# Expert weights of a two-layer mixture-of-experts trunk: three 1 MB transfers per expert, in rows of 8192 bytes, in place of six of 512 KB

## The chip, the cores and the metric

The kernel runs on 1 core of one Trainium2 chip. The metric is the device time of one execution in microseconds (us), median of several runs. One core has TensorE (PE, with its weight loads as PEld), VectorE (DVE), ScalarE (ACT), GpSimd (POOL), SyncE (SP, which here issues the plain DMA transfers) and 16 DMA engines that all queues share.

## The reference, cut to what matters

Two layers over 256 latent and 256 context tokens of width 1024. Each layer has a mixing part (a state-space layer, attention, an mLSTM) and a mixture of experts, which is the part that matters here:

```python
scores = sigmoid(h @ router_w)                  # 64 experts, 8 groups of 8
top_e  = top 8 experts of a token, out of its 4 best groups, by scores + router_bias
gate   = scores[top_e] / sum * 2.5
y      = sum over a token's 8 experts of  gate * ((silu(h @ w_gate[e]) * (h @ w_up[e])) @ w_down[e])
y     += shared expert (same form, for all tokens)
```

`w_gate` and `w_up` are 1024 x 256 per expert, `w_down` is 256 x 1024, all float32: 3 MB per expert (MB in sizes of transfers and slots means 2^20 bytes), 64 experts in each of the 2 layers. Layer 0 routes 512 tokens, layer 1 only the 256 latent ones.

## The kernel before, in words

**Weights in memory.** `prep` (line 101) packs each expert as [128 partitions, 6144]: for k = 0 to 7 the 512 columns of gate and up for the k-th 128 rows of the input, then two blocks of 1024 columns of the down projection. Line 162 cuts this into six chunks of [128, 1024], each contiguous: chunks 0 to 3 are gate and up (two k each), chunks 4 and 5 are down.

**The ring.** `moe` (line 1919) allocates `ring` (line 1931): slots of 4096 bytes per partition, so of 512 KB, 13 of them in layer 0 and 18 in layer 1. One transfer fills one slot. Transfers go round the slots in a fixed order: transfer q goes to slot q modulo the number of slots, and so has to wait until the use of transfer q minus that number is over.

**Units and ranks.** The program counts tokens per expert and sorts the experts by it; the r-th is "rank r". `plan` (line 203) fixes units of work over ranks, with letters in `ORDER` (line 169): X is one rank in two tiles of 128 rows; A, B and C are two ranks in two tiles; L one rank in one tile; D and M two ranks in one tile; S up to four ranks in one tile, 32 columns of the array each. The order, written by hand, is `MSLBCMCLLMLXDMDAXCAMSLMDXSALCBMXLDD` in layer 0 (35 units) and `BDMCSMSLXLMSCXDSCSSSMSLMSM` in layer 1 (26 units). Units are counted from 0 here (C17 is the C that is unit 17 of layer 0). A tile costs PE the same whether one expert or four share it, but an S needs four experts' bytes.

**Order of loads and of use.** `experts` (line 1692) lists the loads in `seq` (lines 1697 to 1702): for unit i all ranks' chunk 0, then chunk 1, and so on to 3, then chunks 4 and 5 of unit i-1. `load` (line 1706) issues the next of them on SP's queue, with the expert's number read into a register; beyond the first ring-full it is conditional on the expert having tokens. `start_loads` (line 1722) fills the ring at the start of the stage, and from then on `gate_up` (line 1777) and `down` (line 1790) call `load` once for each slot that they have used up.

**Order on PE.** For each unit (loop at line 1824): `gate_up` of unit i, the transposes of unit i+1's inputs (`transp`, line 1746), `down` of unit i-1, then the transposes of unit i's hidden values. In `gate_up`, one chunk of all of the unit's ranks is taken at a time (line 1781), and inside it PE goes over tiles, k and ranks; the `load`s for these slots follow the whole chunk. In `down`, PE takes chunks 4 and 5 of all ranks, and gives all their slots back after the last tile.

**Beside it.** In layer 0 the tokens' rows are gathered by indirect DMA on POOL's queue (`gather`, line 1734, two units ahead); in both layers `down` adds its result rows to `Y` in memory by indirect DMA (line 1808). `spilled` (line 1881) handles tokens over the planned capacities, in a loop that reads the ring as one expert's six chunks; its loop makes no pass on these inputs (the trace has 768 expert transfers, 384 per layer, which is 64 times 6).

Of the kernel before, what the change touches and what calls it, by code (L numbers as in the profile page):

```python
# [10 lines left out]
F32 = mybir.dt.float32  # L11
# [89 lines left out]
def prep(inp):  # L101
    f = {k: np.asarray(v) for k, v in inp.items()}
    L = DEPTH
    o = {}
# [54 lines left out]
        dn = np.moveaxis(wd.reshape(*lead, 2, 128, 1024), -3, -2).reshape(*lead, 128, 2048)  # L159
        return np.concatenate([gu, dn], -1)  # L160

    o["exp_w"] = pack(f["exp_w_gate"], f["exp_w_up"], f["exp_w_down"]).reshape(L * 64, 128, 6, 1024).transpose(0, 2, 1, 3)
    o["sh_w"] = pack(f["sh_w_gate"], f["sh_w_up"], f["sh_w_down"])
    o["cst"] = CST
    return {k: np.ascontiguousarray(v) for k, v in o.items()}
# [84 lines left out]
class Trunk:  # L250
# [1441 lines left out]
    def experts(self, l, units, mq, rp, ring, merge):  # L1692
# [3 lines left out]
        part = lambda u, cs: [(u, r, c) for c in cs for r in u["ranks"]]  # L1696
        seq = []
        for i, u in enumerate(units):
            seq += part(u, range(4))
            if i:  # L1700
                seq += part(units[i - 1], (4, 5))
        seq += part(units[-1], (4, 5))
        regs = {}
        state = dict(load=0, use=0)

        def load():
            q = state["load"]
            if q >= len(seq):
                return
            u, r, c = seq[q]  # L1710
            state["load"] += 1
            dst = ring[:, q % NR, :]
            if c == 0:
                vl = lambda at, mx, why: nc.values_load(self.idt[0:1, at:at + 1], engines=[ET.SP], min_val=0, max_val=mx,
                                                        skip_runtime_bounds_check_because=why)
                regs[r] = (vl(r, 63, "an expert's number"), vl(64 + r, 512, "a count of tokens") if q + 24 >= NR else None)
            e, n = regs[r]

            kw = {} if q < NR else dict(cond=n > 0)
            nc.sync.dma_start(dst, wt[l * 64:(l + 1) * 64][ds(e, 1), c].rearrange("e p f -> (e p) f"), **kw)  # L1720
# [56 lines left out]
        def gate_up(u):  # L1777
            for t in u["tiles"]:
                t["gu"] = self.bank("gu")
            for c in range(4):  # L1780
                ws = [use() for _ in u["ranks"]]
                for t in u["tiles"]:
                    for b in range(2):
                        for j, r, kw in pieces(u, t):
                            nc.tensor.matmul(t["gu"][r, :], t["xt"][:, 2 * c + b, r], ws[j][:, b * 512:(b + 1) * 512],  # L1785
                                             start=c == 0 and b == 0, stop=c == 3 and b == 1, **kw)
                for _ in ws:
                    load()

        def down(u):  # L1790
            nr = len(u["ranks"])
            ws = [use() for _ in range(2 * nr)]
            for t in u["tiles"]:
                po = [self.bank("dn") for _ in range(2)]
                for b in range(2):
                    for n in range(2):
                        for j, r, kw in pieces(u, t):
                            nc.tensor.matmul(po[n][r, :], t["ht"][:, b, r], ws[b * nr + j][:, n * 512:(n + 1) * 512],  # L1798
                                             start=b == 0, stop=b == 1, **kw)
                m = t["m"]  # L1800
                xo = rp.tile([128, D], F32, name="xo", bufs=4)
                nc.scalar.activation(xo[0:m, 0:512], po[0][0:m], AF.Identity, scale=t["gc"][0:m])  # L1802
                v.tensor_scalar(out=xo[0:m, 512:1024], in0=po[1][0:m], scalar1=t["gc"][0:m], scalar2=None, op0=OP.mult)  # L1803
                if l and u is units[-1]:
                    t["xo"] = xo
                    continue
                for (_, _, col, _, cap), si in zip(t["segs"], t["si"]):
                    nc.gpsimd.indirect_dma_start(out=self.Y[l], out_offset=bass.IndirectOffsetOnAxis(ap=si[0:cap], axis=0),  # L1808
                                                 in_=xo[col:col + cap], in_offset=None, compute_op=OP.add,
                                                 bounds_check=TOK[l] - 1, oob_is_err=False)  # L1810
            for _ in range(2 * nr):
                load()

        n = len(units)
# [66 lines left out]
    def spilled(self, l, fT, acc, sw, rp, ring, tiles):  # L1881
# [5 lines left out]
        with tc.For_i(0, n, 1) as q:  # L1887
            vl = lambda at, why: nc.values_load(self.ovl[0:1, ds(q + at, 1)] if at else self.ovl[0:1, ds(q, 1)], engines=[ET.SP], min_val=0,
                                                max_val=63, skip_runtime_bounds_check_because=why)
            e, r = vl(0, "an expert's number"), vl(64, "a rank")  # L1890
            w = ring[:, 0:6, :]
            for c in range(6):
                nc.sync.dma_start(w[:, c], d["exp_w"][l * 64:(l + 1) * 64][ds(e, 1), c].rearrange("e p f -> (e p) f"))
            co = rp.tile([128, nt], F32, name="spc")
            nc.sync.dma_start(co, self.cod[l][ds(r, 1), :nt * 128].rearrange("o (i p) -> (o p) i", p=128))
            for i in range(nt):
                gu = self.bank("gu")
                for k in range(8):
                    nc.tensor.matmul(gu, fT[:, k, i * 128:(i + 1) * 128], w[:, k // 2, (k % 2) * 512:(k % 2) * 512 + 512], start=k == 0, stop=k == 7)
                sg = rp.tile([128, 256], F32, name="sg", bufs=3)  # L1900
                h = rp.tile([128, 256], F32, name="hh", bufs=3)
                nc.scalar.activation(sg, gu[:, 0:256], AF.Silu)
                v.tensor_tensor(out=h, in0=gu[:, 256:512], in1=sg, op=OP.mult)
                ps = self.bank("hT")
                ht = rp.tile([128, 2, 128], F32, name="hT", bufs=4)
                for b in range(2):
                    self.tpose(ps[:, b * 128:(b + 1) * 128], h[:, b * 128:(b + 1) * 128])
                v.tensor_copy(ht, ps[:, 0:256].rearrange("p (b n) -> p b n", b=2))
                for n2 in range(2):
                    po = self.bank("dn")  # L1910
                    for b in range(2):
                        nc.tensor.matmul(po, ht[:, b], w[:, 4 + b, n2 * 512:(n2 + 1) * 512], start=b == 0, stop=b == 1)
                    a = acc[:, i, n2 * 512:(n2 + 1) * 512]
                    t = sw[:, 4 + n2, 0:512]
                    v.scalar_tensor_tensor(out=t, in0=po, scalar=co[:, i:i + 1], in1=sw[:, 2 if tiles[i] >= 2 else 3, n2 * 512:(n2 + 1) * 512],
                                           op0=OP.mult, op1=OP.mult)
                    v.tensor_tensor(out=a, in0=a, in1=t, op=OP.add)

    def moe(self, l, mq, fT, sw, lg, tiles, spare):
# [5 lines left out]
        with ExitStack() as es:  # L1925
            rp = es.enter_context(self.tc.tile_pool(name=f"moe{l}", bufs=1))
            if l == 0:
                self.xg = [rp.tile([128, D], F32, name=f"xg{i}") for i in range(5)]
                for x in self.xg:
                    nc.gpsimd.memset(x, 0.0)  # L1930
            ring = rp.tile([128, 18 if last else 13, 1024], F32, name="ring")
            self.xn = 0
            merge = self.merging(l, acc, sw, spare, tiles)
            for i, t in enumerate(tiles[:3]):
# [98 lines left out]
```

## Time and profile before

| | us |
|---|---|
| median of 3 runs | 1990.86 (1983.97 to 1991.81) |
| the profiled execution's own time | 1989.93 |
| its span in the profile | 1988.1 |
| PE busy | 1802.0 (91%) |
| PEld busy | 851.0 (43%) |
| DVE, ACT, POOL busy | 813.2, 379.5, 456.1 |
| DMA over the span | 524.16 MB, mean 264 GB/s |

The expert stage of layer 0 runs from about 392 us (first load issued) to 1085 us, that of layer 1 from about 1428 us to 1948 us. PE's busy time is a union of matmul durations; matmuls of different 32-column groups overlap, so the same busy time can hold more or less work. The share of DMA is the time that packets took, over 16 engines; it can pass 100%, as packets on one engine overlap a little.

### The profile page before, as it was taken

What the parts mean: (1) busy time and instruction counts of PE and PEld (TensorE: products, weight loads), DVE (VectorE), ACT (ScalarE), POOL (GpSimd) and SP (SyncE); (2) the same over time, 40 slices, a digit from 0 to 9 for tenths busy, and PEclk for the clock granted to TensorE, in tenths of its full rate; (3) what the DMA queues carried; (4) which work ended last, traced back from release to release, by engine and by line L of the source; (5) the groups of instructions that cost most, each with busy time, mean ns of one, the idle gap of its engine ahead of it and who ended that gap; (6) DMA issues with size and microseconds to landing.
All of it is one profiled execution on the core that took longest, in us unless ns stands there. A gap on an engine that the chain in (4) does not pass through costs nothing. (4 is left out here: it accounts for less than half of the span.)

```text
span 1988.1 us, 29110 instructions
## 1 busy us (share of the span) xinstructions
PE 1802.0 (91%) x10161; PEld 851.0 (43%) x10161; DVE 813.2 (41%) x2298; ACT 379.5 (19%) x739; POOL 456.1 (23%) x453
## 2 busy tenths in 40 slices
PE   6998999879999999899997178899899999999992
PEld 2554665523334333233332055665543354433340
DVE  6856664731223432222121598764731222312113
ACT  2245331201111111001111313341301011110000
POOL 3120211232223232332221551002101211111223
PEclk7999999989999999999999588999999999999996
DMA  8442567399999999999997423256499999899672
GB/s 321 140 96 101 178 250 293 116 319 358 298 326 340 360 323 293 386 377 339 344 297 232 163 75 64 75 213 258 182 372 343 398 353 358 304 385 355 234 261 69
DMA packets 153922, 524.16 MB, mean 264 GB/s; under 512 B 28787, under 2 KB 37939, under 8 KB 145068
## 3 DMA queue, kind: packets, MB, share of 16 engines
q1 hardware_dynamic: 135228, 480.36, 65.1%
q0 software_dynamic: 18544, 41.90, 9.5%
q8 instruction: 82, 1.34, 0.3%
q14 instruction: 68, 0.56, 0.1%
HBM read 531.12 MB, written 47.61 MB: 291 GB/s over the span
## 5 line engine op out<-in xcount | busy, mean ns | idle before, releaser
L1785 PE MATMUL gu<-ring,xT 128*32 128x512 f32 (+5 forms) x2896 | 645.7, 602 | 18.2 <-DMA ring<-in_exp_w 17.7
L1785 PEld LDWEIGHTS gu<-ring,xT 128*32 128x32 f32 (+5 forms) x2896 | 193.7, 129 | 399.3 <-issue 321.2
L1798 PE MATMUL dn<-ring,hT 128*32 128x512 f32 (+5 forms) x1448 | 330.0, 597 | 4.8 <-DMA ring<-in_exp_w 4.0
L1808 POOL DMA_INDIRECT Y<-xo,gi x79 | 119.9, 1518 | 610.8 <-DMA Y<-xo,gi 140.5
L1681 DVE TENSOR_TENSOR hh<-gu,sg 128x256 f32<-128x256 f32 (+4 forms) x86 | 36.5, 424 | 523.2 <-ACT sg L1680 503.7
L1798 PEld LDWEIGHTS dn<-ring,hT 128*32 128x32 f32 (+5 forms) x1448 | 103.1, 128 | 183.2 <-issue 155.7
L1808 POOL DMA_INDIRECT Y<-xo,si x66 | 91.0, 1379 | 302.6 <-DMA Y<-xo,gi 217.4
L1803 DVE TENSOR_SCALAR xo<-dn,gc 128x512 f32<-128x512 f32 (+5 forms) x80 | 60.0, 751 | 229.0 <-PE dn L1798 215.6
L1680 ACT ACTIVATE sg<-gu 128x256 f32<-128x256 f32 (+4 forms) x86 | 32.8, 384 | 586.6 <-PE gu L1785 586.3
L443 PE MATMUL pT<-hT,w 128*128 128x512 f32 (+1 forms) x288 | 120.4, 572 | 4.3 <-DMA w<-in_w_mm 2.7
L1760 PEld LDWEIGHTS <-fb 128*128 128x128 bf16 x1536 | 86.3, 99 | 41.9 <-issue 41.9
L1802 ACT ACTIVATE xo<-dn,gc 128x512 f32<-128x512 f32 (+5 forms) x80 | 55.0, 687 | 253.3 <-PE dn L1798 239.2
L1760 PE MATMUL xT<-oneh,fb 128*128 128x128 bf16 (+4 forms) x1536 | 94.6, 220 | 0.0
L1392 PE MATMUL yo<-w,cat 128*128 128x512 f32 x192 | 83.4, 594 | 0.8 <-DMA w<-in_w_out 0.8
L1762 DVE COPY xT<-xT 128x512 f32<-128x512 f32 (+5 forms) x80 | 53.2, 670 | 70.0 <-PE xT L1760 37.2
L1762 ACT COPY xT<-xT 128x512 f32<-128x512 f32 (+5 forms) x80 | 45.8, 573 | 185.4 <-PE xT L1760 135.3
L443 PEld LDWEIGHTS pT<-hT,w 128*128 128x128 f32 x288 | 56.0, 200 | 58.0 <-issue 47.5
L290 PE MATMUL hT<-cst,xt 128*128 128x128 f32 x64 | 14.6, 404 | 59.3 <-ACT xt L1982 55.2
L451 PE MATMUL pN<-w,hT 128*128 128x256 f32 (+2 forms) x256 | 65.0, 414 | 3.0 <-DVE va L1268 3.0
L342 PE MATMUL ada<-w,sil 128*32 128x512 f32 x384 | 57.9, 649 | 10.4 <-DMA w<-in_ada_w 10.4
L1742 POOL DMA_INDIRECT xg<-fd,gi x48 | 50.3, 1047 | 48.2 <-PE xT L290 19.0
L451 PEld LDWEIGHTS pN<-w,hT 128*128 128x128 f32 x256 | 49.2, 203 | 19.9 <-issue 5.2
(546 smaller groups left out, 2071.1 us busy)
## 6 DMA issues: line engine op xcount, KB each, us to landing
ring<-in_exp_w SPq DMA_DIRECT2D x768, 512.0 KB
w<-in_ada_w SPq DMA_DIRECT2D x48, 1024.0 KB
w<-in_w_out SPq DMA_DIRECT2D x8, 1024.0 KB
sw<-in_sh_w SPq DMA_DIRECT2D x2, 3072.0 KB
w<-in_w_uv SPq DMA_DIRECT2D x4, 1024.0 KB
Y<-zeros SPq DMA_DIRECT2D x8, 512.0 KB
w<-in_w_mm SPq DMA_DIRECT2D x4, 1024.0 KB
w<-in_w_qk SPq DMA_DIRECT2D x4, 768.0 KB
```

Of the source, the lines that this page charges most:

```text
L342: nc.tensor.matmul(ps[32 * q:32 * q + 32, :], self.sil[:, k, :], t[:, q * 512:(q + 1) * 512], start=k == 0, stop=k == 7, tile_position=(0, ...
L443: self.nc.tensor.matmul(ps[base:base + m, n0:NT], w[k][:, col:col + m], hT[:, k, n0:NT], start=k == 0, stop=k == 7)
L451: self.nc.tensor.matmul(ps[:, :n], hT[:, k, i * 128:(i + 1) * 128], w[k][:, col:col + n], start=k == 0, stop=k == 7)
L1392: nc.tensor.matmul(st[at][n], cb[:, i * 128:(i + 1) * 128], wo[n][b], start=b == 0, stop=b == 7)
L1742: nc.gpsimd.indirect_dma_start(out=x[col:col + cap], out_offset=None, in_=self.fd, in_offset=bass.IndirectOffsetOnAxis(ap=si[0:cap], axis= ...
L1760: nc.tensor.matmul(o, self.fb[i][:, z, cs], t["oh"][:, i, 0:m], start=at == 0, stop=at + 1 == len(parts))
L1762: (nc.scalar.copy if hh else v.tensor_copy)(o, a)
L1785: nc.tensor.matmul(t["gu"][r, :], t["xt"][:, 2 * c + b, r], ws[j][:, b * 512:(b + 1) * 512], start=c == 0 and b == 0, stop=c == 3 and b == ...
L1798: nc.tensor.matmul(po[n][r, :], t["ht"][:, b, r], ws[b * nr + j][:, n * 512:(n + 1) * 512], start=b == 0, stop=b == 1, **kw)
L1802: nc.scalar.activation(xo[0:m, 0:512], po[0][0:m], AF.Identity, scale=t["gc"][0:m])
L1803: v.tensor_scalar(out=xo[0:m, 512:1024], in0=po[1][0:m], scalar1=t["gc"][0:m], scalar2=None, op0=OP.mult)
L1808: nc.gpsimd.indirect_dma_start(out=self.Y[l], out_offset=bass.IndirectOffsetOnAxis(ap=si[0:cap], axis=0), in_=xo[col:col + cap], in_offset ...
```

## The change

The six chunks of an expert become three of twice the size ([128, 2048], rows of 8192 bytes per partition): chunks 0 and 1 are gate and up with four k each, chunk 2 is the down projection. The ring's slots double in size: 6 in layer 0 (12 of the old size, where there were 13), 9 in layer 1 (18 of the old size, as before). Loads, uses and conditions follow; the matmuls and their number stay.

```diff
-    o["exp_w"] = pack(...).reshape(L * 64, 128, 6, 1024).transpose(0, 2, 1, 3)
+    o["exp_w"] = pack(...).reshape(L * 64, 128, 3, 2048).transpose(0, 2, 1, 3)
...
         for i, u in enumerate(units):
-            seq += part(u, range(4))
+            seq += part(u, (0, 1))
             if i:
-                seq += part(units[i - 1], (4, 5))
-        seq += part(units[-1], (4, 5))
+                seq += part(units[i - 1], (2,))
+        seq += part(units[-1], (2,))
...
-                regs[r] = (vl(r, 63, "an expert's number"), vl(64 + r, 512, "a count of tokens") if q + 24 >= NR else None)
+                regs[r] = (vl(r, 63, "an expert's number"), vl(64 + r, 512, "a count of tokens") if q + 12 >= NR else None)
...
-            for c in range(4):
+            for c in range(2):
                 ws = [use() for _ in u["ranks"]]
                 for t in u["tiles"]:
-                    for b in range(2):
+                    for b in range(4):
                         for j, r, kw in pieces(u, t):
-                            nc.tensor.matmul(t["gu"][r, :], t["xt"][:, 2 * c + b, r], ws[j][:, b * 512:(b + 1) * 512],
-                                             start=c == 0 and b == 0, stop=c == 3 and b == 1, **kw)
+                            nc.tensor.matmul(t["gu"][r, :], t["xt"][:, 4 * c + b, r], ws[j][:, b * 512:(b + 1) * 512],
+                                             start=c == 0 and b == 0, stop=c == 1 and b == 3, **kw)
...
-            ws = [use() for _ in range(2 * nr)]
+            ws = [use() for _ in range(nr)]
...
-                            nc.tensor.matmul(po[n][r, :], t["ht"][:, b, r], ws[b * nr + j][:, n * 512:(n + 1) * 512],
+                            nc.tensor.matmul(po[n][r, :], t["ht"][:, b, r], ws[j][:, b * 1024 + n * 512:b * 1024 + (n + 1) * 512],
...
-            for _ in range(2 * nr):
+            for _ in range(nr):
                 load()
...
-            ring = rp.tile([128, 18 if last else 13, 1024], F32, name="ring")
+            ring = rp.tile([128, 9 if last else 6, 2048], F32, name="ring")
```

`spilled` reads the same bytes through the new shape (three transfers into slots 0 to 2).

## Rows read from the trace of the kernel before

**Rows 1.** Layer 0's expert stage, 392 to 1085 us: queues (q1 SP's, q0 POOL's), packets, MB, share.

```profile
DMA packets 67595, 229.20 MB, mean 331 GB/s; under 512 B 11718, under 2 KB 11718, under 8 KB 67545
q1 hardware_dynamic: 53808, 195.73, 75.7%
q0 software_dynamic: 13737, 32.84, 20.1%
```

**Rows 2.** DMA queues in layer 1's expert stage, 1428 to 1948 us.

```profile
q1 hardware_dynamic: 45020, 163.68, 80.9%
q0 software_dynamic: 4224, 8.26, 8.5%
```

**Rows 3.** Windows: PE, PEld, DVE, ACT, POOL busy (instructions), PEclk, DMA share, GB/s.

```profile
598.00:806.00 208.00, 205.70 (x1066) 82.43 (x1068) 66.56 (x182) 29.99 (x54) 61.37 (x50) 1.00 0.98 333
806.00:922.00 116.00, 106.79 (x507) 38.45 (x507) 28.87 (x94) 12.14 (x22) 39.23 (x32) 0.99 1.01 369
...
1786.00:1838.00 52.00, 50.30 (x355) 18.22 (x348) 9.82 (x37) 5.14 (x9) 9.63 (x7) 1.00 0.94 364
```

**Rows 4.** SP's own waits in layer 0's expert stage, 405 to 1090 us: total, times, longest.

```profile
SPq L1720 <- PE gu L1785: 143.8, 80, 13.5
SPq L1720 <- DMA ring<-in_exp_w: 115.8, 121, 3.5
```

**Rows 5.** PE in order of time, layer 0: start, duration, what, [idle before it <-releaser].

```profile
683.72 1.06 PE L1785 MATMUL gu<-ring,xT 128*32 128x512 f32 x6 [1.00 <-DMA ring<-in_exp_w]
...
805.90 3.62 PE L1785 MATMUL gu<-ring,xT 128*32 128x512 f32 x20
...
814.00 0.51 PE L290 MATMUL xT<-cst,xg 112*128 112x112 f32 x3
...
824.30 4.50 PE L1785 MATMUL gu<-ring,xT 128*32 128x512 f32 x12 [2.44 <-DMA ring<-in_exp_w]
...
1081.64 1.90 PE L1798 MATMUL dn<-ring,hT 128*32 128x512 f32 x10 [0.60 <-DMA ring<-in_exp_w]
```

**Rows 6.** DMA queue q1 from 10 to 22 us (above) and 1440 to 1452 us (below).

```profile
DMA packets 868, 5.08 MB, mean 423 GB/s; under 512 B 96, under 2 KB 224, under 8 KB 292
q1 hardware_dynamic: 867, 5.07, 102.1%
...
q1 hardware_dynamic: 1373, 5.01, 102.2%
```

**Rows 7.** SP's issues from 1833 us (layer 1, experts without tokens); DMA in 40 slices, 1833 to 1843 us.

```profile
1833.74 7.49 SPq L1720 DMA_DIRECT2D ring<-in_exp_w  x12
...
GB/s 197 213 180 115 98 66 66 66 33 33 0 16 0 0 33 0 0 0 0 0 0 0 0 66 0 0 0 0 0 0 0 0 82 213 295 344 492 393 262 262
```

**Rows 8.** PE in order of time: half a gate_up of a four-expert unit without waits.

```profile
1522.10 3.64 PE L1785 MATMUL gu<-ring,xT 128*32 128x512 f32 x32
```

**Rows 9.** SP's issues and the DMA engines' rate in 40 slices, 1634 to 1644 us.

```profile
1640.42 2.05 SPq L1720 DMA_DIRECT2D ring<-in_exp_w  x2
...
GB/s 311 377 377 377 344 229 197 115 147 115 131 246 49 82 66 164 98 147 131 147 164 148 164 180 49 0 0 0 0 147 295 197 377 393 393 262 98 82 164 262
```

**Rows 10.** PE in order of time, units C17 and A18; SP's issues from 391 to 753.8 us.

```profile
742.29 15.12 PE L1785 MATMUL gu<-ring,xT 128*128 128x512 f32 x80
...
759.15 7.03 PE L1798 MATMUL dn<-ring,hT 128*128 128x512 f32 x16
...
766.56 15.12 PE L1785 MATMUL gu<-ring,xT 128*128 128x512 f32 x80
...
L1720 SPq DMA_DIRECT2D ring<-in_exp_w x196: 13/333/899, 391.8 to 753.7; - x196
```

**Rows 11.** The start of layer 0's stage: SP's first issue after the first ring-full; PE's first gate_up.

```profile
416.85 0.33 SPq L1720 DMA_DIRECT2D ring<-in_exp_w  x1
...
415.73 7.08 PE L1785 MATMUL gu<-ring,xT 128*64 128x512 f32 x30
```

More of the change, by code (lines that the diff above doesn't have):

```diff
@@ L160, in pack @@
         return np.concatenate([gu, dn], -1)
-    o["exp_w"] = pack(f["exp_w_gate"], f["exp_w_up"], f["exp_w_down"]).reshape(L * 64, 128, 6, 1024).transpose(0, 2, 1, 3)
+    o["exp_w"] = pack(f["exp_w_gate"], f["exp_w_up"], f["exp_w_down"]).reshape(L * 64, 128, 3, 2048).transpose(0, 2, 1, 3)
     o["sh_w"] = pack(f["sh_w_gate"], f["sh_w_up"], f["sh_w_down"])
@@ L1890, in spilled @@
             e, r = vl(0, "an expert's number"), vl(64, "a rank")
-            w = ring[:, 0:6, :]
-            for c in range(6):
+            w = ring[:, 0:3, :]
+            for c in range(3):
                 nc.sync.dma_start(w[:, c], d["exp_w"][l * 64:(l + 1) * 64][ds(e, 1), c].rearrange("e p f -> (e p) f"))
@@ L1898, in spilled @@
                 for k in range(8):
-                    nc.tensor.matmul(gu, fT[:, k, i * 128:(i + 1) * 128], w[:, k // 2, (k % 2) * 512:(k % 2) * 512 + 512], start=k == 0, stop=k == 7)
+                    nc.tensor.matmul(gu, fT[:, k, i * 128:(i + 1) * 128], w[:, k // 4, (k % 4) * 512:(k % 4) * 512 + 512], start=k == 0, stop=k == 7)
                 sg = rp.tile([128, 256], F32, name="sg", bufs=3)
@@ L1911, in spilled @@
                     for b in range(2):
-                        nc.tensor.matmul(po, ht[:, b], w[:, 4 + b, n2 * 512:(n2 + 1) * 512], start=b == 0, stop=b == 1)
+                        nc.tensor.matmul(po, ht[:, b], w[:, 2, b * 1024 + n2 * 512:b * 1024 + (n2 + 1) * 512], start=b == 0, stop=b == 1)
                     a = acc[:, i, n2 * 512:(n2 + 1) * 512]
```

## The prediction, made before the changed kernel ran

> **What bounds the kernel now.** The change touches the two expert stages only, so I went to those and asked first whether DMA or PE ends the waits there. The DMA queues of layer 0's stage: over 693 us (392 to 1085) the weights' queue takes 75.7% of the 16 engines and the gathers and scatters 20.1%, together 95.8% [rows 1]. DMA has 4.2% x 693 = 29 us to spare in the whole stage. Layer 1 has more: 80.9% + 8.5% = 89.4% of 520 us, so 55 us [rows 2]. Next the windows: in 806 to 922 us the DMA share is 1.01 while PE, with 106.79 of 116 us, has idle time; from 598 to 806 both are nearly full (0.98, and 205.70 of 208 us) [rows 3]. Layer 0 is a balance: units that need many bytes per tile (S, M, D) are fed from what was loaded ahead while PE worked on two-tile units (A, B, C, X). The ring is what carries this lead from the one to the other. SP's own waits say so too: its loads wait 143.8 us for gate_up matmuls to free a slot and 115.8 us for earlier transfers [rows 4]; the first is a full ring, the second a saturated queue. Last, PE in order of time shows where the lead runs out: PE stands for ring transfers at 683.72 (a D), at 824.30 (the S that began at 805.90) and at 1081.64, in the very last down [rows 5]. There, whatever DMA lost before comes out as time.
>
> **Part by part.**
>
> *Longer rows.* Does a 1 MB transfer in 8192-byte rows move faster? The trace has both. From 10 to 22 us the queue carries mainly 1 MB transfers of `ada_w`: of 868 packets, 576 are of 8 KB or more, and 5.07 MB take 102.1%. From 1440 to 1452 us it is 512 KB expert transfers: 5.01 MB take 102.2% [rows 6]. Per 100% of the engines that is 5.07 / (1.021 x 12 us) = 414 GB/s against 409, or 1.3%. On layer 0's weights this is at most 1.3% of 75.7% of 693 us = 7 us, on layer 1's 1.3% of 80.9% of 520 us = 5 us, of which only the stretches count where DMA is the limit. I take -3 us in layer 0 and -1 in layer 1; bounds 0 and -12 together.
>
> The Trainium skill ("DMA: Bandwidth & Descriptors", Bandwidth) asks for 1 MiB per transfer or more and fits about 2 us plus the bytes over 436 GB/s for one transfer of GpSimd's queue; an estimate from that page is 3.2 us for 512 KB and 4.4 us for 1 MB, so 2.0 us saved per pair and, with 187 pairs in layer 0, up to 370 us. The trace disagrees: on SP's queue, transfers of 512 KB already follow each other at 5.01 MB per 12 us, one each 1.25 us [rows 6].
>
> *Half as many issues.* SP's work per load halves. In layer 0 SP waits for PE or DMA anyway [rows 4], so 0. In layer 1 the loads of experts without tokens are skipped at a cost: 12 issues from 1833.74 take 7.49 us, and the engines' rate falls to zero for some 5 us of that [rows 7]. Half as many would save up to 3 us there; PE is nearly covered, so I take -1, bounds -3 and 0.
>
> *Four-expert units with six slots (layer 0).* A chunk of an S now holds 4 of 6 slots, where it held 4 of 13. After its fourth transfer lands, only two more are under way: 2 x 1.05 MB, which is 5.0 us at 419 GB/s, or 7.4 us at the weights' mean pace in this stage (195.73 MB in 693 us [rows 1]). New loads start only when PE has done the chunk: 3.64 us for the 32 matmul records that it consists of [rows 8], then 0.9 us from issue to data (1640.42 to the first filled slice at about 1641.3 [rows 9]), then an unseen landing-to-PE delay, which I bound by 0 and 2.5 us (2.44 us is the longest wait in [rows 5]). So 4.5 to 7.0 us to cover with 5.0 to 7.4: a hole of 0 to 2 us. Three S units have three chunks each: 9 x 1 = +9 us, bounds 0 and +18. Two-expert units hold 2 of 6 and leave four transfers as cover (10 us): 0. In layer 1 S leaves 5 of 9 (12.5 us): 0.
>
> *Less lead (layer 0).* Take C17 and A18. Before A18 stand 32 ranks' gate_ups and 30 ranks' downs, 4 x 32 + 2 x 30 = 188 loads, so A18's eight are loads 189 to 196; the 196th was issued at 753.7 [rows 10]. It belongs to the last quarter of A18's gate_up, which starts at 766.56 + 11.34 = 777.9: issued 24.2 us ahead. In the changed kernel A18 has loads 95 to 98, and load q waits for the slot of q-6. Load 98 waits for C17's third load, which is used until the end of C17's gate_up, 742.29 + 15.12 = 757.4; it is needed at A18's half, 766.56 + 7.56 = 774.1: 16.7 us ahead. Load 96 waits for half of C17's gate_up (749.9), for use at 766.56: 16.7 again. Loads 95 and 97 keep about 24 us. And each lands 1.25 us later, being twice as long. So the lead falls by 1 to 9 us, by load; I take 5, about the mean (1.25 + 7.5 / 2). It is paid where the lead then runs out to nothing: three such places show in [rows 5], +15 us; bounds 0 (other lead covers it) and 4 x 9 = +36.
>
> *Start and end.* Thirteen loads went out at once, the 14th at 416.85, after the first quarter of the first gate_up [rows 11]. Now six (12 old ones) do, and the seventh waits for its half: 415.73 + 3.54 = 419.3, +2.4 us. At the end of layer 0 PE had 10 records, 1.90 us, to do after the last landing [rows 5]; now the whole last down waits for its slots, 32 records, some 3.6 us: +1.7. Together +4, bounds 0 and +6.
>
> *Layer 1.* Same bytes in 9 slots; what is lost is the coarser freeing and landing, 1.25 to 4 us where the lead runs out. The windows show one such stretch plainly, 1786 to 1838 (share 0.94, PE 50.30 of 52 us [rows 3]); I take two places at 2 us: +4, bounds 0 and +10.
>
> *Order on PE.* The program's builder already puts input transposes inside an S's gate_up (814.00 [rows 5]) and may put them elsewhere now. I take 0 and put the risk in the range.
>
> **The sum.** -3 - 1 - 1 + 9 + 15 + 4 + 4 = +27 us. The profiled execution took 1989.9 us (span 1988.1 us and 1.8 around it), 0.9 below the median of the runs; 1990 + 27 = **2017 us**. All low ends: 1990 - 15 = 1975. All high ends: 1990 + 18 + 36 + 6 + 10 = 2060.
>
> **The rivals.**
>
> *Longer rows win (faster).* The mechanism: per-packet and per-transfer overhead falls where DMA has no time to spare, layer 0, and nothing is lost since PE is covered anyway. For it: 95.8% of DMA's time is taken [rows 1]. By clean streams it gives 12 us, 1978. If longer rows also won back what the weights' queue loses beside scatters (195.73 MB at 75.7% of 693 us is 373 GB/s against 414), it would be 9.9% of 525 us = 52 us, 1938. It decides as soon as the holes and the lost lead together cost less than about 2 us. Against it: two nearly equal rates [rows 6]. This is the way in which the rule of the Trainium skill on 1 MiB would come true here, and its chance is this rival's.
>
> *PE hides it (no change).* The waits before PE are short and the lost lead is rebuilt in the next two-tile unit; then the gain of 5 and a loss of 5 to 15 us leave 1985 to 2000. For it: PE busy 205.70 of 208 us in 598 to 806 [rows 3]. Against: DMA's 29 us to spare is all there is for rebuilding.
>
> *The ring of six is far too small (much slower).* Every S chunk opens 2 us, every drain costs 9 us: the high ends, 2060. For it: 13 old slots hold one whole two-expert unit plus one load, 6 new ones just the unit. Against: scatters fill part of a hole.
>
> **How the numbers follow.** A measurement of this kernel can tell about 0.5%, 10 us, from no change: 1981 to 2001. My forecast's own case, slower by 10 to 50 us, has 0.63; the ring far too small, beyond that, 0.10; PE hides it 0.15; faster 0.12. So slower 0.73, same 0.15, faster 0.12. The range 1983 to 2048 leaves out the faster case and most of the largest losses, together about 0.2.
>
> **What would show it.** Right: layer 0's stage longer than 693 us by about 25 us with its weights' queue at a share below 75.7%; pauses of 1 to 2 us in DMA inside S units; SP waiting more for PE and hardly for earlier transfers; PE's waits for the ring longer at the D of 683, the S of 806 and the end; layer 1 longer by under 5 us. Wrong: layer 0's share of the weights' queue per byte falls by several per cent; or PE's waits stay as they are; or the extra time lies in layer 1 or outside the expert stages.

## The result, and the profile after

The changed kernel takes **2014.45 us** (median of 4 runs, 2010.37 to 2017.12) against 1990.18 us for the kernel before in the same comparison: ratio 1.012, 95% interval 1.0100 to 1.0139, so 24 us slower. The profiled execution took 2010.37 us, 20.4 us more than the profiled one of before (1989.93).

**Where the time lies.** First the windows over the two expert stages, from the first gate_up to the last down, before (first two rows) and after (next two). Columns as in [rows 3]: PE, PEld, DVE, ACT, POOL busy with their instructions, granted clock, DMA share, GB/s.

```profile
403.00:1084.00 681.00, 658.80 (x3180) 251.20 (x3178) 174.46 (x496) 84.64 (x155) 183.38 (x147) 0.99 0.96 331
1440.00:1948.00 508.00, 503.73 (x3518) 212.03 (x3516) 116.42 (x382) 54.38 (x100) 92.18 (x65) 1.00 0.90 333
```

```profile
403.00:1095.00 692.00, 659.82 (x3178) 257.45 (x3177) 174.53 (x494) 84.51 (x155) 181.98 (x145) 0.97 0.93 324
1454.00:1971.00 517.00, 502.48 (x3520) 214.94 (x3518) 116.80 (x382) 54.77 (x100) 91.47 (x65) 0.99 0.85 325
```

Layer 0's stage grew by 11 us and layer 1's by 9. PE's busy time did not grow: its idle time went from 22.2 to 32.2 us in layer 0 (681 - 658.80, 692 - 659.82) and from 4.3 to 14.5 in layer 1, +20.2 in all. So in this profile the loss is, net, PE standing still (two changes of its busy time cancel; see the last section), with DMA less busy than before (0.93 for 0.96, 0.85 for 0.90): both wait for each other more.

**What PE stands for.** The waits of the whole execution that end with a ring transfer, before and after (total, times, longest). The PE rows hold PE's own idle time; the PEld rows are waits of weight loads, which overlap PE.

```profile
PE gu L1785 <- DMA ring<-in_exp_w: 17.7, 21, 2.4
PE dn L1798 <- DMA ring<-in_exp_w: 4.0, 4, 1.6
```

```profile
PE gu L1785 <- DMA ring<-in_exp_w: 34.4, 22, 4.3
PE dn L1798 <- DMA ring<-in_exp_w: 7.8, 6, 2.9
```

42.2 us for 21.7: +20.5, as much as the profiled execution lost. There are hardly more waits (28 for 25), but each is longer: the longest is 4.3 us for 2.4. A second profile of the changed kernel (run `changed_again` below) has 41.3 us of these waits, so +19.6; what is said below of single places is compared with it.

**What SP stands for**, layer 0's expert stage of the kernel after, 403 to 1100 us, beside [rows 4]:

```profile
SPq L1720 <- PE gu L1785: 326.1, 69, 22.5
SPq L1720 <- DMA ring<-in_exp_w: 0.4, 1, 0.4
```

Before, SP's loads were held by a full ring for 143.8 us and by a saturated queue for 115.8. Now they practically never wait for the queue: nearly every load is issued late, when a slot comes free.

**The DMA queues** of the kernel after, layer 0 (390 to 1096 us) and layer 1 (1442 to 1971 us), beside [rows 1, 2]:

```profile
DMA packets 40748, 229.05 MB, mean 324 GB/s; under 512 B 8706, under 2 KB 8706, under 8 KB 16896
q1 hardware_dynamic: 27024, 195.72, 72.2%
q0 software_dynamic: 13680, 32.76, 19.9%
```

```profile
q1 hardware_dynamic: 22556, 163.67, 76.5%
```

The same bytes in half the packets. The engines' time for the weights of layer 0 is 72.2% of 706 us = 510 us, against 75.7% of 693 = 525: 2.8% less per byte. Part of it is the row length: two profiles of a kernel below, with 1 MB transfers in rows of 4096 bytes, have 73.6% and 74.0% in the same stretch, and the second profile of the changed kernel 72.0%. So longer rows do make the same bytes cheaper, by 2 to 3%. No time came of it that the experiments can tell.

**The places.** PE in order of time, kernel after: the S that began at 805.90 before [rows 5] (first five rows), the next S (S25), the end of layer 0, and the S that is unit 6 of layer 1.

```profile
802.96 1.04 PE L1785 MATMUL gu<-ring,xT 128*32 128x512 f32 x2
...
808.61 1.04 PE L1785 MATMUL gu<-ring,xT 128*32 128x512 f32 x2 [1.77 <-DMA ring<-in_exp_w]
810.87 5.32 PE L1785 MATMUL gu<-ring,xT 128*32 128x512 f32 x28 [1.22 <-DMA ring<-in_exp_w]
...
820.89 1.43 PE L1785 MATMUL gu<-ring,xT 128*32 128x512 f32 x2 [3.16 <-DMA ring<-in_exp_w]
823.37 6.02 PE L1785 MATMUL gu<-ring,xT 128*32 128x512 f32 x26 [1.05 <-DMA ring<-in_exp_w]
...
910.27 3.63 PE L1785 MATMUL gu<-ring,xT 128*32 128x512 f32 x28
918.23 6.39 PE L1785 MATMUL gu<-ring,xT 128*32 128x512 f32 x30 [4.33 <-DMA ring<-in_exp_w]
...
1083.66 1.92 PE L1798 MATMUL dn<-ring,hT 128*32 128x512 f32 x12 [1.39 <-DMA ring<-in_exp_w]
...
1583.18 3.63 PE L1785 MATMUL gu<-ring,xT 128*32 128x512 f32 x28 [1.41 <-DMA ring<-in_exp_w]
...
1593.02 5.21 PE L1785 MATMUL gu<-ring,xT 128*32 128x512 f32 x26 [1.41 <-DMA ring<-in_exp_w]
```

Two things are to be seen. The waits stand inside S units, as forecast. And some of the matmul groups behind a wait are longer than the 3.64 us that the same half of an S takes without one [rows 8]: 6.02, 6.39, 5.21. Windows of the kernel after, around S25's wait:

```profile
906.00:914.00 8.00, 7.90 (x60) 3.16 (x57) 4.88 (x17) 1.17 (x2) 3.52 (x3) 1.00 0.93 294
914.00:918.20 4.20, 0.00 (x0) 0.00 (x0) 0.00 (x0) 0.00 (x0) 0.00 (x0) 0.86 0.98 303
918.20:925.00 6.80, 6.77 (x31) 1.67 (x32) 0.00 (x0) 0.27 (x1) 2.43 (x2) 0.59 0.81 282
925.00:940.00 15.00, 15.00 (x64) 6.01 (x63) 3.15 (x8) 1.49 (x3) 1.58 (x1) 1.00 1.00 368
```

After 4.2 us without a matmul the granted clock is 0.59 in the next 6.8 us, so most of that stretch ran at the lower of the two levels (1.2 GHz), and then it is 1.00 again. The wait of 4.33 us therefore cost 4.33 + (6.39 - 3.64) = 7.1 us. In the second profile of the changed kernel PE waits at the same place for 1.01 us only, and the same 30 matmuls behind it take 3.63 us:

```profile
919.52 3.63 PE L1785 MATMUL gu<-ring,xT 128*32 128x512 f32 x30 [1.01 <-DMA ring<-in_exp_w]
```

So this 7.1 us is a matter of one execution, and no fixed price of the change.

Set against the kernel before, unit by unit, by the ends of their gate_ups and downs: 2.9 us ahead at the end of unit 18, 0.6 behind after S20, 3.8 after M22, 10.6 after S25 (before it 3.6; the difference is the 7.1 just worked out), 8.1 at unit 29, 11.0 at the end of layer 0; in layer 1, 13.2 behind at the end of its first gate_up, 8.9 after M5's, 18.5 after S6's, and 22.7 at its last down. In between, each unit of two ranks in two tiles (A, B, C) gives 0.7 us back. The second profile has some of this and not the rest: 0.9 ahead at the end of unit 18, 3.2 behind after S20, 8.2 before S25 and 9.2 after it, 8.2 at unit 29, 8.6 at the end of layer 0. M5 and S6 are alike in both (+9.5 and +9.5). What stands between the last down of layer 0 and the first gate_up of layer 1 differs most: 357.1 us before, 360.0 and 367.4 after.

### The profile page after: what moved, and what is told of

The parts are those of the page before. It is cut to its first block, busy times and chain, and to the rows that moved or that the text cites. A ratio compares the mean times of both kernels' runs of the same rounds, so it can differ in the third digit from the quotient of the medians.

```text
span 2008.5 us, 27600 instructions
## 1 busy us (share of the span) xinstructions
PE 1801.8 (90%) x10161; PEld 860.1 (43%) x10161; DVE 811.1 (40%) x2298; ACT 379.1 (19%) x739; POOL 455.8 (23%) x453
## 5 line engine op out<-in xcount | busy, mean ns | idle before, releaser
L1785 PE MATMUL gu<-ring,xT 128*32 128x512 f32 (+5 forms) x2896 | 631.0, 616 | 34.5 <-DMA ring<-in_exp_w 34.4
L1785 PEld LDWEIGHTS gu<-ring,xT 128*32 128x32 f32 (+5 forms) x2896 | 199.2, 131 | 409.5 <-issue 337.3
L1798 PE MATMUL dn<-ring,hT 128*32 128x512 f32 (+5 forms) x1448 | 346.8, 605 | 8.7 <-DMA ring<-in_exp_w 7.8
L1798 PEld LDWEIGHTS dn<-ring,hT 128*32 128x32 f32 (+5 forms) x1448 | 107.2, 129 | 197.7 <-issue 167.9
```

Source lines behind the costliest of these rows:

```text
L1785: nc.tensor.matmul(t["gu"][r, :], t["xt"][:, 4 * c + b, r], ws[j][:, b * 512:(b + 1) * 512], start=c == 0 and b == 0, stop=c == 1 and b == ...
L1798: nc.tensor.matmul(po[n][r, :], t["ht"][:, b, r], ws[j][:, b * 1024 + n * 512:b * 1024 + (n + 1) * 512], start=b == 0, stop=b == 1, **kw)
```

## The experiments

The expectations name theories by letters. **A** is the prediction's: the ring is smaller and coarser, S units and drained leads pay for it, rows matter little. **B**: the long rows do give back some 15 us per stage, and the coarse ring costs that much more. **C**, formed on the first results: the lost slot, slots that land and come free as a whole, and PE's coarser passes each have their price. **D**: it is the coarser passes on PE that cost. Ratios are against runs of the kernel before on the same chip (medians 1990.21, 1991.24 and 1989.76 us in the three groups of runs). All kernels here compute the whole of the reference.

### Small transfers into large slots

The changed kernel's ring (6 and 9 slots of 1 MB) and its order on PE, but two transfers of 512 KB in rows of 4096 bytes fill a slot.

```diff
-            nc.sync.dma_start(dst, wt[...][ds(e, 1), c]..., **kw)
+            for h in range(2):
+                nc.sync.dma_start(dst[:, h * 1024:(h + 1) * 1024], wt[...][ds(e, 1), 2 * c + h]..., **kw)
```

> The changed kernel's ring (6 and 9 slots of 1 MB, freed whole), but each slot filled by two transfers of 512 KB in rows of 4096 bytes. Theory A (the prediction's: long rows give little, under 5 us): 24 to 30 us over the kernel before, as the changed kernel (+24). Theory B (from the changed kernel's trace: long rows give back some 15 us in each expert stage's DMA time, and the coarse ring costs more than was predicted): 35 to 50 us over before. The weights' queue takes 75 to 76% of layer 0's stage per its length under B's reading of rows, against 72.2% in the changed kernel.

2000.72 us, ratio 1.0051 (1.0034 to 1.0068): +10, not +24. So something in the 1 MB transfers costs, and the smaller ring with its coarse passes is less than half of the loss. A large slot here is not wholly coarse, though: its halves are tracked apart. In C17, whose gate_up starts at 741.03, SP issues the next load of the first rank's first half after 5.6 us and that of its second half after 7.3, when PE is through with the slot:

```profile
L1721 SPq DMA_DIRECT2D ring<-in_exp_w x2: 333/333/333, 746.6 to 748.3; - x2
```

The second rank's first half gains nothing, as SP issues in order: its load follows at 749.0.

### Large transfers in short rows

1 MB transfers as in the change, out of the old packing, so in rows of 4096 bytes; and once more in a later group, beside the changed kernel itself.

```diff
-            nc.sync.dma_start(dst, wt[...][ds(e, 1), c]..., **kw)
+            nc.sync.dma_start(dst.rearrange("p (h f) -> p h f", h=2),
+                              wt[...][ds(e, 1), 2 * c:2 * c + 2].rearrange("e h p f -> (e p) h f"), **kw)
```

> The changed kernel with transfers of 1 MB as it has, but in rows of 4096 bytes (two per partition). If the length of rows gives the gain (theory B): as the kernel with two 512 KB transfers per slot, 35 to 50 us over before. If the number or the size of transfers gives it: as the changed kernel, 24 us over before. Theory A (no gain to speak of): 24 to 30 us.

2009.68 us, 1.0107 (1.0080 to 1.0135). The second time:

> Transfers of 1 MB in rows of 4096 bytes again, now beside the changed kernel and with more rounds. If long rows give nothing that can be measured: within 3 us of the changed kernel. If they give what the saturated stretch shows: 3 to 10 us slower than it.

> The changed kernel itself, beside the other three on one chip: 20 to 28 us over before. If rows of 8192 bytes give what the trace of a saturated stretch shows (2.7% more bytes), it is 3 to 10 us faster than the same with rows of 4096 bytes.

Rows of 4096 bytes: 2014.75 us, 1.0110 (1.0084 to 1.0137). Rows of 8192 (the changed kernel): 2014.03 us, 1.0113 (1.0096 to 1.0129). The length of the rows makes no difference to the time that these runs can tell; by their intervals they would not see one under some 6 us either way. In the profiles PE's part alone, from a layer's first gate_up to its last down, is shorter with long rows: 680.8 and 679.2 us in layer 0 and 515.9 and 516.1 in layer 1, for 683.0, 689.5, 519.9 and 521.7; what lies between and behind the two stages is longer by about as much (398.1 and 404.9 us for 389.1 and 395.0), and why is not shown. The length of the rows does show in the queue. The weights' queue in a stretch of 56 us in which DMA is saturated and PE waits (units 4 to 7 of layer 1), first the kernel after, 1560 to 1616 us, then rows of 4096 bytes, same stretch:

```profile
q1 hardware_dynamic: 3052, 22.14, 94.0%
```

```profile
q1 hardware_dynamic: 5602, 21.56, 94.7%
```

2.7% more bytes (22.14 / 21.56) beside 7.5% and 7.8% for the scatters; in the profiles of the later group it is 1.9% (21.71 / 21.31). In 56 us that is 1.1 to 1.5 us of transfers, and such stretches are few; it is lost in the scatter of the runs. Theory B, which wanted 35 to 50 us over before with short rows, falls in that size; a gain of a few us from long rows is not excluded.

### One slot fewer, small transfers

The kernel before with 12 slots in layer 0, the bytes of the changed ring.

```diff
-            ring = rp.tile([128, 18 if last else 13, 1024], F32, name="ring")
+            ring = rp.tile([128, 18 if last else 12, 1024], F32, name="ring")
```

> The kernel before with 12 slots of 512 KB in layer 0, the bytes that the changed kernel has, nothing else. Both theories: 0 to 5 us over before, as the lost slot is 1.25 us of lead at each of three places. Rival (the lost 512 KB itself is the cause): 15 us or more over before, all in layer 0.

1997.46 us, 1.0029 (1.0017 to 1.0042): +6 by the ratio, +7 by the medians, a little over what was expected. The missing 512 KB alone are a quarter of the loss.

### Coarse passes on PE, small slots

The kernel before, whose gate_up takes two chunks at a time: four k per tile and rank, as in the change, but out of 512 KB slots, whose loads follow after both. Once in all units, once only in units with more than one tile and more than one rank (A, B, C).

```diff
-            for c in range(4):
-                ws = [use() for _ in u["ranks"]]
+            n = 2
+            for c0 in range(0, 4, n):
+                ws = [[use() for _ in u["ranks"]] for _ in range(n)]
```

In the second kernel the count depends on the unit:

```diff
+            n = 2 if len(u["tiles"]) > 1 and len(u["ranks"]) > 1 else 1
```

> The kernel before (13 and 18 slots, transfers of 512 KB) with the changed kernel's order on PE: gate_up takes two chunks at a time, so four k of one tile before the next tile. Theories A and B are given up: after the first four runs theory C says that the +24 us of the changed kernel are one lost slot (+7), transfers of 1 MB that land and are freed as a whole (+10 to 14), and the coarser passes of PE less what its order gains (+3). By C this kernel is 0 to 5 us over before. Rival D (the coarse passes are what costs, and the number of transfers little): 10 us or more over before.

> The kernel before, with two chunks at a time in gate_up only for units of two ranks in two tiles (A, B, C; 10 units in layer 0, 4 in layer 1), whose gate_up takes 0.7 us less in the changed kernel's trace. By theory C 5 to 9 us under before. Rival D: what such a unit gains is lost where the lead next runs out, 0 to 5 us over before.

1989.93 us, 0.9993 (0.9981 to 1.0005), and 1989.17 us, 0.9988 (0.9977 to 0.9999). Theory D falls: coarse passes cost nothing, although a first chunk's slots in A, B and C then come free after the second tile's turn with it, later than before. In A, B and C they even save PE time. C17 in the second of these kernels, PE in order of time:

```profile
743.13 14.45 PE L1787 MATMUL gu<-ring,xT 128*128 128x512 f32 x80
```

It was 15.12 us with two k at a time [rows 10]; the matmuls are the same, but PE goes only half as often from one tile to the other and back. That it is the change of shape that costs is argued, not isolated: these units have a first tile of one piece of 128 columns and a second one of pieces of 32 or 64, while X31, with two whole tiles, takes 14.00 us before and in the kernel with pairs in all units alike. Thirteen units have this form (nine in layer 0, where the expectation counts ten, and four in layer 1), so PE saves 13 x 0.67 = 8.7 us, of which 1 or 2 arrive, not the 5 to 9 expected: by difference, the rest turns into waiting for DMA.

### Seven slots of 1 MB

The changed kernel with a seventh slot in layer 0; the room comes from one buffer fewer of another tile. First the result tile `xo` (4 to 3 in layer 0), then the transposed input `xT`.

```diff
-                xo = rp.tile([128, D], F32, name="xo", bufs=4)
+                xo = rp.tile([128, D], F32, name="xo", bufs=4 if l else 3)
...
-            ring = rp.tile([128, 9 if last else 6, 2048], F32, name="ring")
+            ring = rp.tile([128, 9 if last else 7, 2048], F32, name="ring")
```

> The changed kernel with 7 slots of 1 MB in layer 0; the room comes from one of the four result tiles that wait for their scatter (three in layer 0). Theory A: an S then leaves three transfers under way (7.5 us of cover for at most 7.0), no hole, and the lead grows by 2.5 us: 5 to 10 us over before. Theory B: the same 5 to 10 us, with layer 0's stage shorter than before's by some us and layer 1's 10 to 13 us longer still. Rival (not the number of slots but that they are freed whole): 18 us or more over before.

2006.93 us, 1.0074 (1.0053 to 1.0095), but the buffer taken away has a price of its own. PE near the end of layer 0, and the longest waits of 1040 to 1095 us, in this kernel:

```profile
1078.29 4.50 PE L1798 MATMUL dn<-ring,hT 128*104 128x512 f32 x5 [7.09 <-ACT sg L1680]
```

```profile
ACT xo L1802 <- DMA Y<-xo,si: 27.3, 2, 14.6
DVE xo L1803 <- DMA Y<-xo,si: 27.1, 2, 14.5
```

With three result tiles ACT and DVE stand behind the scatters, and PE behind them. So the other donor:

> The changed kernel with 7 slots of 1 MB in layer 0, the room now from one of four tiles for transposed inputs in layer 0 (the first try with 7 slots took a result tile, and PE waited some 10 us for those at the end of layer 0). By theory C the lost slot is more than made good in layer 0, and layer 1 stays 10 to 13 us longer: 3 to 10 us over before. Rival: 7 slots of 1 MB are no better than 6, 20 us over before.

2008.10 us, 1.0083 (1.0061 to 1.0105): some 6 us better than the changed kernel (about as much as the intervals allow to tell), and still 17 slower than before, with 14 old slots' worth of ring against 13; 3 to 10 were expected. Size alone does not repair the change.

### Freed as a whole, landed by halves

From the first experiment (two transfers per slot) one step further: PE's order inside a slot is changed so that the first half is in use until the end, k in the order 0, 2, 3, 1, and in `down` the (b, n) pairs as 00, 10, 11, 01. The second half's load stands behind the first's in SP's queue, so neither half is loaded anew before PE is through with the slot.

```diff
-                    for b in range(4):
+                    for b in (0, 2, 3, 1):
...
-                for b in range(2):
-                    for n in range(2):
+                for at, (b, n) in enumerate(((0, 0), (1, 0), (1, 1), (0, 1))):
```

> The kernel with two 512 KB transfers per slot, with an order of PE that uses a slot's first half first and also last (k 0, 2, 3, 1 of four; in down the same), so that both halves are freed only at the end, while each still lands by itself. If the price of the 1 MB transfer is that it is freed as a whole: 18 to 25 us over before, like the changed kernel. If it is that it lands as a whole: 8 to 14 us over, like the kernel with two transfers per slot (+10).

2012.05 us, 1.0111 (1.0094 to 1.0128): +22, where the same transfers into the same slots had +10. The order in which PE touches the halves costs 12 us (by the two intervals 7 to 17), half of the loss, and brings the time to that of the changed kernel (1.0113 in the same group) with no 1 MB transfer in it. In C17, whose gate_up starts at 750.38 here, both loads of the first rank's slot go out after 7.3 us, at the end of the chunk; and SP's waits for earlier transfers in 403 to 1100 us, a sign of loads that are issued ahead of the queue, fall from the first row below (halves freed singly) to the second:

```profile
L1721 SPq DMA_DIRECT2D ring<-in_exp_w x2: 333/333/333, 757.7 to 758.4; - x2
...
SPq L1721 <- DMA ring<-in_exp_w: 81.6, 93, 3.1
SPq L1721 <- DMA ring<-in_exp_w: 30.9, 39, 3.0
```

One reservation: this order also needs the second half a quarter of the slot's work earlier, an estimated 0.9 us in C17 (14.45 us over 16 passes of one k over one tile), where the load goes out 1.7 us later. The 12 us are the price of both, and no run sets them apart; in the changed kernel, too, a slot is needed whole as well as freed whole.

By the last down of one profile each, the two kernels with halves are further apart (29.4 and 9.8 us behind the kernel before), but what follows that down took 33 us here, 38 in the changed kernel and 40 before. A stage does not end with PE's last down: POOL's scatters follow, one behind the landing of the other, as here in the kernel before, after layer 0's last down has ended at 1083.54:

```profile
1094.48 1.39 POOL L1808 DMA_INDIRECT Y<-xo,si  x1 [3.98 <-DMA Y<-xo,gi]
```

Counted with them, from layer 0's first gate_up to layer 1's and from there to the end, this kernel is 15.0 and 6.3 us behind the kernel before, the one with halves freed singly 6.9 and 4.3, the changed kernel 14.7 and 6.5 (second profile 20.5 and 6.1): in the order of the medians. Its losses do not all stand where the changed kernel's do: in layer 0 it loses 5 to 7 us around D14 and nothing in S25.

What it does to DMA is seen in the first 110 us of layer 1's stage, where PE is never short and the ring should fill up for the S units behind. Windows of the same units in the kernel before, with halves freed singly, with halves freed as a whole, and after:

```profile
1440.00:1556.00 116.00, 115.19 (x826) 48.70 (x824) 28.41 (x100) 12.46 (x23) 13.34 (x9) 1.00 0.98 361
```

```profile
1445.00:1557.00 112.00, 111.19 (x828) 49.43 (x826) 29.11 (x103) 12.63 (x24) 13.25 (x9) 1.00 0.99 362
```

```profile
1455.00:1566.00 111.00, 110.19 (x825) 48.98 (x824) 29.02 (x102) 12.53 (x24) 13.34 (x9) 1.00 0.97 354
```

```profile
1454.00:1565.00 111.00, 110.19 (x826) 49.06 (x824) 28.31 (x100) 12.44 (x23) 12.40 (x9) 1.00 0.92 346
```

DMA's share is 0.98, 0.99, 0.97 and 0.92. At 0.92 DMA stood still for 8% of 111 us = 9 us, with no slot free to load into. In M5 and S6, right behind this stretch, the last three lose 6.6, 8.3 and 9.5 us against the kernel before: the same order, but not in proportion to the share, so that pauses of DMA in this stretch are not the whole of the loss there.

### Layer 1 alone

1 MB transfers and nine slots in layer 1, layer 0 as before (a factor per layer in place of the constants).

```diff
+CH = (1, 2)
...
-            for c in range(4):
+            for c in range(4 // z):
...
-                    for b in range(2):
+                    for b in range(2 * z):
```

> The change in layer 1 alone (9 slots of 1 MB); layer 0 has 13 slots of 512 KB and its old order. The prediction had +2 us net for layer 1 (+4 lead, -1 rows, -1 issues). The changed kernel's one trace has about +10 there, most of it at the units M and S after the first S. By the trace: 8 to 13 us over before. By the prediction's sum: 1 to 5 us.

1997.90 us, 1.0040 (1.0024 to 1.0056): +8. By difference layer 0 has about 16 of the 24. Layer 1's ring has as many bytes as before, so these 8 us are not the price of a smaller ring.

### A kernel that beats both

Coarse passes in A, B and C, small transfers, and the room of one `xT` buffer used for a 14th slot of 512 KB in layer 0.

```diff
-                xt = self.xtp.tile([128, 8, 128], F32, name="xT", bufs=4)
+                xt = self.xtp.tile([128, 8, 128], F32, name="xT", bufs=4 if l else 3)
...
-            ring = rp.tile([128, 18 if last else 13, 1024], F32, name="ring")
+            ring = rp.tile([128, 18 if last else 14, 1024], F32, name="ring")
```

> The kernel before with two chunks at a time in gate_up for units of two ranks in two tiles, and 14 slots of 512 KB in layer 0 (the room from one of four tiles for transposed inputs). If a slot is worth 7 us here as between 12 and 13: 10 to 16 us under before. If the lead of 13 slots is enough: as without the extra slot, 5 to 9 us under before.

**1982.88 us**, 0.9960 (0.9946 to 0.9974): 8 us faster than before (10 to 16 were expected), 31 faster than the change. Against the same kernel with 13 slots it gains 6, as the step from 12 to 13 did. Layer 0's stage, and PE's waits for the ring in the whole execution:

```profile
403.00:1071.00 668.00, 651.07 (x3177) 253.67 (x3175) 174.07 (x494) 84.09 (x155) 181.64 (x145) 0.99 0.98 337
```

```profile
PE gu L1787 <- DMA ring<-in_exp_w: 14.3, 20, 2.7
PE dn L1800 <- DMA ring<-in_exp_w: 2.2, 3, 1.6
```

16.5 us of waits for 21.7 before (13.6 for 18.9 in layer 0's stage alone), DMA at 0.98 for 0.96: more lead, DMA hardly ever idle in this stage.

## Why the prediction was right, point by point

Forecast +27 us (2017), measured +24 (2014.45): the sign, the size and the main cause, a smaller and coarser ring, held. Of the terms of the sum some were mis-sized, in both directions, and that the total came within 3 us is in part luck.

- **Longer rows, -3 - 1.** The runs show no difference, 2014.03 and 2014.75 us with rows of 8192 and 4096 bytes, to within some 6 us, so that the 4 us forecast are neither borne out nor excluded. The rate is better, by 1.9% and 2.7% in a saturated stretch rather than the 1.3% of [rows 6]. The rule of the Trainium skill ("DMA: Bandwidth & Descriptors", Bandwidth), 1 MiB or more per transfer, brings nothing here that the runs can tell: 512 KB against 1 MB into the same slots, both freed as a whole, is 1.0111 against 1.0113.
- **Half as many issues, -1.** No run isolates it. SP now stands 195.1 us in layer 1 for gate_up (63.7 before), so issuing is no limit there.
- **Four-expert units with six slots, +9.** Right in kind, wrong in how it is spread. The gate_ups of S1, S20 and S25 take 1.5, 3.5 and 7.0 us longer than before in the first profile, 2.9, 4.1 and 0.9 in the second: 12 and 8 in all, around the 9. In S20 the mechanism shows: the third load of its second half goes out at 815.4, when PE is at the end of the first half (the 28 records from 810.87), and PE gets that transfer at 820.89.

```profile
L1720 SPq DMA_DIRECT2D ring<-in_exp_w x4: 333/333/362, 815.4 to 817.5; - x4
```

  In S25 two of the four experts have no tokens; their slots pass without a transfer (SP's issues for them take 79 to 99 ns, those that move data 333 to 343), a case that the prediction did not count. It is so in both profiles, so it does not by itself explain the 7.0 of the first; there only 4.33 us are waiting and 2.75 the lower clock behind it. The sum left the clock out altogether.
- **Less lead, +15 at three places.** The mechanism is the one that the runs bear out: slots used as a whole, so issued later (+12 between the two kernels with halves, with the reservation made there), and fewer bytes of them (+6 for 512 KB). The size is too large and the places are partly wrong. At the D of 683.72 I expected 5 us; the kernel after is 2.2 us ahead there (0.1 behind in the second profile). PE had saved up to 0.7 us in each B and C before it, which the term "order on PE, 0" missed. S20 to S25 is where it was paid: from 2.9 ahead to 10.6 behind in the first profile, from 0.9 ahead to 9.2 behind in the second, S units included.
- **Start and end, +4.** The start: DMA does pause, as these windows show, before and then after (columns as above):

```profile
410.00:420.00 10.00, 10.00 (x55) 4.35 (x54) 5.94 (x27) 0.59 (x1) 2.36 (x3) 1.00 0.75 223
```

```profile
410.00:420.00 10.00, 10.00 (x51) 3.81 (x51) 5.73 (x27) 0.59 (x1) 3.14 (x3) 1.00 0.36 104
```

  The share falls from 0.75 to 0.36, but the first S ends only 0.7 us later than before (1.4 in the second profile); the price is small. The end: unit 29 to the last down goes from 8.1 to 11.0, +2.9, in the first profile and from 8.2 to 8.6 in the second; I had +1.7 here and 5 of the lead.
- **Layer 1, +4 and net +2.** This is far off by its proportion: alone, layer 1 measures +8 where +2 was forecast. I took the places from DMA's share, with 1786 to 1838 as the plain one; that stretch (C16, S17) costs 4 us. The largest, M5 and S6 at 1556 to 1580 before, I did not see, since PE hardly waited there before: 0.20 to 0.45 us at a time, five times in a row, the longest of them in this row of PE in order of time of the kernel before:

```profile
1575.35 1.04 PE L1785 MATMUL gu<-ring,xT 128*32 128x512 f32 x2 [0.45 <-DMA ring<-in_exp_w]
```

  Those short waits were the sign that the lead ran out exactly there.
- **Sum by layer.** Forecast +25 in layer 0 and +2 in layer 1; measured about +16 and +8. Two errors that offset each other brought the total nearer than its terms were.
- **The rivals.** Longer rows winning: excluded by the two runs on row length. PE hiding it: excluded by the time; the 0.7 us that each A, B and C gives back is PE's own saving and not lead rebuilt. The ring far too small: excluded by the time, 2014 against 2060.
- **The signs.** Seen: SP waiting for PE (326.1 for 143.8) and not for transfers (0.4 for 115.8), share of the weights' queue below 75.7%, longer waits at the S of 806. Weakly or in one profile only: pauses of DMA inside S units (in S20 its share falls to 0.91 from 811.0 to 816.2 us, between 1.02 and 1.03), longer waits at the end. Not seen: layer 0 longer by 25 (11 in the profile, 16 by the runs), the D of 683, layer 1 under 5. The sign I gave for wrong, cheaper bytes by several per cent, came in part (2 to 3%) and yet was no loss to the theory: it shows DMA's price per byte, not what ends PE's waits.

**The ledger of the 24 us** as the runs give it: one 512 KB slot fewer in layer 0, about +6; slots used and freed only as a whole, about +12; length of rows, 0; coarse passes alone, -1 or so. Together 17, each term to within 3 to 6 us, so that the remaining 7 are hardly beyond the scatter; they are not isolated. Part of them may be in the large slots with halves freed singly (+10 against +6 for the lost slot), which differ from the 12-slot kernel in layer 1 too; how much is the whole landing of a 1 MB transfer was not tried by itself.

## What to carry to other kernels

When a ring of buffers carries a lead from compute-heavy to transfer-heavy stretches, its grain counts as well as its size: a slot holds bytes that are done with until its last byte is. Using and giving back slots only as a whole cost some 12 us here, and the rounding down of the ring from 13 small slots to 12 another 6. Before making transfers larger, look at whether the queue already streams (SP waiting for earlier transfers, two equal rates in different transfer sizes): where it does, as here, there is little to gain. Take a second profile before a single place is explained: 7 us in one unit here were 0.9 in the next execution. Look for the loss where short waits follow each other behind a stretch without any, and count the matmuls behind a long wait at the clock that the profile shows behind such waits.

## What the runs showed of the hardware that was not expected

- **A wait of PE can cost more than its length.** After 4.2 us without a matmul the granted clock was 0.59 for the next 6.8 us, and 30 matmuls took 6.39 us where such a half took 3.64 [rows 8]. After waits of 3.16 and 1.05 us, in S20, it was 0.59 from 823.4 to 829.3 too:

```profile
816.20:823.40 7.20, 2.50 (x8) 0.30 (x8) 0.00 (x0) 0.00 (x0) 3.43 (x3) 0.86 1.03 386
823.40:829.30 5.90, 5.90 (x26) 1.24 (x26) 0.00 (x0) 0.00 (x0) 0.62 (x2) 0.59 1.00 362
```

  PE's busy time in the two stages is the same before and after (1162.53 and 1162.30 us) although thirteen gate_ups got 0.67 us shorter; by difference the lower clock added about 8 us. Behind a wait of 1.01 us, at the same place in the second profile, 30 matmuls took 3.63 us: no loss.
- **Fewer turns between two tiles of unlike pieces save PE time**: 15.12 to 14.45 us for the same gate_up of two ranks in two tiles; two whole tiles (X31) take 14.00 us either way.
- **Rows of 8192 bytes carried 2.7% and 1.9% more than rows of 4096** in a saturated stretch beside scatters (two pairs of profiles), more than the 1.3% of [rows 6], and no time came of it that the runs can tell.
- **Two transfers into one buffer are not one large transfer**: their halves are tracked apart and come free apart (loads 1.7 us apart in C17), worth some 12 us here, until the order of use ties them together.
